# Neighbourhood keys stored as 64, meta, 384, meta, 64: nine transposes a head, and probabilities written over the biases

## The chip, the core and the metric

One core of a Trainium2 chip runs the whole program. Its engines are TensorE (PE, matmuls out of SBUF into PSUM), VectorE (DVE), ScalarE (ACT), GpSimd (POOL) and SyncE (SP), whose queue issues nearly all DMAs. Each engine takes its instructions in the order in which they were written into the program, and waits for others by semaphores. The metric is the time of one execution on the device in microseconds (us), the median of the runs.

## What is computed

Two layers of an encoder over 512 tokens (a grid of 8 rows and 64 columns) and 16 meta tokens, width 1024. A layer projects its normalised input with one large matrix, and its columns feed grouped-query attention (GQA), neighbourhood attention, and gates. The change touches neighbourhood attention: 8 heads of 64. A grid token sees the tokens of all 8 rows in a window of 16 columns, with a learned bias for each relative place, and the 16 meta keys; a meta token sees the meta keys alone.

```python
s_win  = einsum('bchd,bicjhd->bhcij', q_row, k_win) * scale + bias
s_meta = einsum('bchd,bmhd->bhcm', q_row, km) * scale
p = softmax(concatenate([s_win, s_meta], -1))
o = einsum('bhcij,bicjhd->bchd', p_win, v_win) + einsum('bhcm,bmhd->bchd', p_meta, vm)
o_meta = einsum('bhqm,bmhd->bqhd', softmax(s_mm), vm)
```

## The kernel before

Everything is float32. Each operand of a matmul is split into a high and a low part (`split`: a copy on ACT, a subtraction on DVE; for weights ACT and POOL), and three matmuls stand for one product (`product`, lines 309 to 311). The outer loop runs over chunks of 128 output columns of the projection; within a chunk over one or two ranges of tokens, of 264 or 512 columns, each into one of two PSUM banks (`ps_p`), then evacuated. After each range `tick()` moves two side streams on, one for neighbourhood heads (`side_na`) and one for GQA: a head is a list of steps, each with the number of ticks after the head's start (`NA_AT`). So the attention work is sown between the projections. A scheduler then sets each engine's order from the operations, their priorities (`tc.high_priority`) and the buffers.

Tokens are ordered by grid column, so a block of 128 queries covers 16 columns, and the keys that it needs are a contiguous run. The four blocks are in `BLK`: where the block's scores lie in a row of 960, its first key, and its number of keys (208, 272, 272, 208). Keys are stored with the 16 meta keys put in three times, 560 in all, so that each block's run holds one copy of them. The bias tile of a head (128 x 960, loaded in step `prepare`) has the same order.

A head's steps (`windowed_head`):

- `scores`: eight matmuls into a tile of two PSUM banks; DVE adds the bias and takes the maximum (line 874) into two tiles `Pb` of the shared set `B`; ACT takes the exponential; DVE and ACT scale.
- `transposes1` and `transposes2`: eight transposes on PE into the banks `ta` and `tb` (two banks, `ps_t`, serve all transposes of the kernel, GQA's `pt` and `ptm` too); `tb` has two narrow ones of 64 columns for the first and the last 64 keys. They are split into `tah`, `tal`, `tbh`, `tbl`; for the narrow ones `split_down` puts the low part on the partitions under the high one.
- `transposes3`: four transposes of 32 columns, one a block, of the stretch that holds its meta keys, into bank `tc`, split into `na` (128 x 512).
- `sums`: nine matmuls of these with the values `VB` into `avb`, then `combine`.

The values of a pair of heads are transposed in three calls (`window_values`): `vtb` (three of 128 tokens), `vtc` (two of 64), `vtd` (one of 32, with the meta tokens). In the rows, `pp` and `y` are projections, `whi` and `wlo` their weights, `vb` and `kb` values and keys of a pair, `S` and `P` GQA's scores and probabilities, `mm` and `tm` those of the meta queries, `avbm` their sum. Line numbers of the change are some 10 to 35 higher.

Of the kernel before, what the change touches and what calls it, by code (L numbers as in the profile page):

```python
# [11 lines left out]
F32 = mybir.dt.float32  # L12
# [14 lines left out]
NKEY = NTOK + 2 * NMETA  # L27
LAST = NTOK - P
HD = 64
# [7 lines left out]
NA_AT = ({"stages": (0, 2, 5, 5, 5, 7), "values": (3, 4, 6)},  # L37
         {"stages": (0, 2, 4, 5, 5, 7), "values": (3, 4, 5)})
# [14 lines left out]
BLK = ((0, 0, 208), (208, 64, 272), (480, 208, 272), (752, 352, 208))  # L53

BLK_META = (176, 112, 112, 176)


def _window_index():

    key = list(range(192)) + [-1] * 16 + list(range(192, 320)) + [-1] * 16 + list(range(320, 512)) + [-1] * 16  # L60
# [31 lines left out]
def trunk_kernel(ctx: ExitStack, tc: tile.TileContext, xT, w, gn, gf, bias, rope, out):  # L92
# [68 lines left out]
    for kind, (cols, n, dt) in {"ga": (256, 1, F32R), "na": (512, 1, F32R), "mm": (NMETA, 1, F32R), "pm": (32, 1, F32)}.items():  # L161
# [264 lines left out]
    for l in range(DEPTH):  # L426
# [197 lines left out]
        def keys_scaled():  # L624
# [46 lines left out]
        def values(v, out, tiles, name):
# [516 lines left out]
```

## Time and profile before

| what | value |
| --- | --- |
| median of 3 runs | 868.41 us (867.76 to 868.47) |
| the profiled execution | 869.61 us |
| its span, first to last instruction | 867.8 us |
| PE busy (matmuls) | 854.8 us, 99%, 5976 instructions |
| DVE busy | 537.2 us, 62% |
| ACT busy | 494.2 us, 57% |
| POOL busy | 365.6 us, 42% |
| chain that ended last | PE 86%, ACT 6%, DVE 4%, DMA 2% |
| PE clock granted | full in all 40 slices |

Busy times of PE count overlapping matmuls, so the share says that the queue is filled and not how fast it is worked off. That is read from the starts in the timeline. The rows are in a section further down.

### The profile page before, as it was taken

What the parts mean: (1) busy time and instruction counts of PE and PEld (TensorE: products, weight loads), DVE (VectorE), ACT (ScalarE), POOL (GpSimd) and SP (SyncE); (2) the same over time, 40 slices, a digit from 0 to 9 for tenths busy, and PEclk for the clock granted to TensorE, in tenths of its full rate; (3) what the DMA queues carried; (4) which work ended last, traced back from release to release, by engine and by line L of the source; (5) the groups of instructions that cost most, each with busy time, mean ns of one, the idle gap of its engine ahead of it and who ended that gap; (6) DMA issues with size and microseconds to landing.
All of it is one profiled execution on the core that took longest, in us unless ns stands there. A gap on an engine that the chain in (4) does not pass through costs nothing.

```text
span 867.8 us, 16234 instructions
## 1 busy us (share of the span) xinstructions
PE 854.8 (99%) x5976; PEld 790.6 (91%) x5976; DVE 537.2 (62%) x1277; ACT 494.2 (57%) x1170; POOL 365.6 (42%) x300
## 2 busy tenths in 40 slices
PE   8999999999999999999999999999999999999997
PEld 8999999999999999999998989898988888888786
DVE  5985667676774574436547656677767646454633
ACT  7645677677774555333445456677767645543432
POOL 5564323443223332544764643334333333334751
PEclk9999999999999999999999999999999999999999
DMA  6364253325112222325555664235422222223602
GB/s 223 99 186 145 93 150 99 106 73 153 49 50 75 62 67 81 98 86 152 148 139 127 171 198 130 79 95 151 145 81 73 86 73 73 87 85 97 206 25 97
DMA packets 64671, 95.76 MB, mean 110 GB/s; under 512 B 22864, under 2 KB 23376, under 8 KB 64592
## 3 DMA queue, kind: packets, MB, share of 16 engines
q1 hardware_dynamic: 63872, 93.66, 36.8%
q8 instruction: 47, 0.77, 0.4%
q10 hardware_dynamic: 720, 1.06, 0.3%
q14 instruction: 32, 0.26, 0.1%
HBM read 76.72 MB, written 4.19 MB: 93 GB/s over the span
## 4 chain that ended last, share of the span: by engine, by line
PE 86%; ACT 6%; DVE 4%; DMA 2%; issue 1%; POOL 0%; SPq 0%; POOLq 0%; ACTq 0%; DVEq 0%
PE pp L311 18%; PE pp L309 18%; PE pp L310 17%; PE y L309 4%; PE y L311 4%; PE y L310 3%; PE av L797 3%; PE pt L124 3%; PE avb L940 2%; PE pf L1115 2%; PE S L525 2%; PE pf L1117 2%; PE pf L1116 1%; PE S L526 1%; DMA x<-in_xT_dram 1%
## 5 line engine op out<-in xcount | busy, mean ns | idle before, releaser
L227 POOL TENSOR_TENSOR wlo<-raw,whi 128x512 fp32r<-128x512 f32 x214 | 285.3, 1337 | 425.4 <-ACT whi L226 341.7
L309 PE MATMUL pp<-hh,whi 128*128 128x264 f32 (+1 forms) x1056 | 334.7, 317 | 0.6 <-ACT qs L461 0.5
L311 PE MATMUL pp<-hh,wlo 128*128 128x264 f32 (+1 forms) x1056 | 329.3, 312 | 0.0
L310 PE MATMUL pp<-hl,whi 128*128 128x264 f32 (+1 forms) x1056 | 328.6, 311 | 0.0
L226 ACT CAST whi<-raw 128x512 fp32r<-128x512 f32 x214 | 131.5, 619 | 152.7 <-PE pp L310 58.3
L311 PEld LDWEIGHTS pp<-hh,wlo 128*128 128x128 f32 x1056 | 198.8, 188 | 10.7
L309 PEld LDWEIGHTS pp<-hh,whi 128*128 128x128 f32 x1056 | 198.6, 188 | 10.1 <-ACT qs L461 1.1
L310 PEld LDWEIGHTS pp<-hl,whi 128*128 128x128 f32 x1056 | 199.3, 189 | 9.0
L750 DVE CUSTOM_DVE_ANT_1 P<-S,r 128x528 f32<-128x528 f32 x64 | 45.1, 704 | 18.5 <-PE S L526 17.6
L183 DVE TENSOR_TENSOR ptl<-pt,pth 128x512 fp32r<-128x512 f32 x64 | 44.0, 689 | 18.0 <-ACT pth L182 17.2
L1012 DVE TENSOR_TENSOR mg<-pp,rbc 128x264 f32<-128x264 f32 (+1 forms) x48 | 24.8, 517 | 43.2 <-PE pp L311 42.7
L754 ACT ACTIVATE P<-P,st 128x528 f32<-128x528 f32 x64 | 47.2, 737 | 1.9
L876 ACT ACTIVATE Pb<-Pb,stb 128x208 f32<-128x208 f32 (+1 forms) x64 | 31.1, 487 | 16.6 <-DVE stb L874 16.3
L124 PE MATMUL pt<-ident,P 128*128 128x128 f32 x256 | 39.3, 275 | 0.6 <-DVE ptl L183 0.4
L182 ACT CAST pth<-pt 128x512 fp32r<-128x512 f32 x64 | 37.2, 583 | 4.2 <-PE pt L124 2.9
L1013 ACT ACTIVATE mg<-mg 128x264 f32<-128x264 f32 (+1 forms) x48 | 23.7, 494 | 24.4 <-DVE mg L1012 24.4
L310 PE MATMUL pp<-mx,whi 128*128 128x264 f32 x128 | 36.6, 286 | 0.0
L309 PE MATMUL pp<-mx,whi 128*128 128x264 f32 x128 | 36.4, 285 | 0.0
L311 PE MATMUL pp<-mx,wlo 128*128 128x264 f32 x128 | 36.3, 284 | 0.0
L797 PE MATMUL av<-pth,VA 128*128 128x256 f32 x128 | 35.0, 296 | 0.0
L756 DVE TENSOR_SCALAR P<-P,st 128x528 f32<-128x528 f32 x64 | 33.7, 527 | 2.1
L797 PE MATMUL av<-ptl,VA 128*128 128x256 f32 x128 | 33.1, 281 | 0.0
(526 smaller groups left out, 1764.3 us busy)
## 6 DMA issues: line engine op xcount, KB each, us to landing
raw<-in_w_dram SPq DMA_DIRECT2D x214, 256.0 KB, 2.7
bias<-in_bias_dram SPq DMA_DIRECT2D x16, 480.0 KB, 4.5
KB<-KB SPq DMA_DIRECT2D x24, 280.0 KB, 4.0
rawl<-in_w_dram SPq DMA_DIRECT2D x16, 256.0 KB, 2.9
x<-in_xT_dram SPq DMA_DIRECT2D x8, 264.0 KB, 6.3
xr<-in_xT_dram SPq DMA_DIRECT2D x8, 264.0 KB, 3.9
Q<-q SPq DMA_DIRECT2D x16, 128.0 KB, 2.9
x1d<-xt SPq DMA_DIRECT2D x32, 64.0 KB, 2.8
```

Of the source, the lines that this page charges most:

```text
L124: nc.tensor.transpose(ps, src, ident[:n, :n])
L182: split_at["hi"] = nc.scalar.copy(hi, src)
L183: split_at["any"] = nc.vector.tensor_sub(lo, src, hi.bitcast(F32))
L226: cast = nc.scalar.copy(hi, raw)
L227: sub = nc.gpsimd.tensor_sub(lo, raw, hi.bitcast(F32))
L309: nc.tensor.matmul(ps, wh, rh[:, a:b], start=i == 0, stop=False)
L310: nc.tensor.matmul(ps, wh, rl[:, a:b], start=False, stop=False)
L311: nc.tensor.matmul(ps, wl, rh[:, a:b], start=False, stop=i == n - 1)
L750: newest["max"] = nc.vector.tensor_tensor_reduce(p[:n].rearrange("p (i k) -> p i k", i=2), S[:n, :, :HALF], scale[:n].unsqueeze(2).to_broa ...
L754: nc.scalar.activation(p[:n], p[:n], AF.Exp, bias=st[:n, 1:2], scale=1.0, accum_out=st[:n, 2:3])
L756: nc.vector.tensor_scalar_mul(p[:n], p[:n], st[:n, 3:4])
L797: nc.tensor.matmul(c["av"], rows2(c["t"][i][0]), c["t"][i][1], start=i == 0, stop=i == 8)
```

## The change

The keys of a pair are stored as 64 tokens, 16 meta, 384 tokens, 16 meta, 64 tokens, 544 in all. Each block's run still holds one copy of the meta keys: the first two blocks use the first copy, the last two the second. In the first and the last block the meta keys lie beside the edge keys, so the two narrow transposes of `tb` take 80 columns, edge and meta together, and their low parts get a tile of their own instead of the lower partitions. In the bias tile the blocks stand in the order 0, 2, 1, 3; the ends of blocks 2 and 1 meet there, with the meta keys of both within 64 columns, and one transpose into `tc` serves both. Its tile `na` has 256 columns; the unwanted rows in it meet zeros in `VB`, made by a mask `inner`.

DVE writes the scores with bias, and ACT the exponentials, over the bias tile itself; the two tiles `Pb` are gone. The values of a pair are evacuated in the new order (`window_scaled`, five instructions for two), and the edges and meta values are transposed in one call (`window_edges`); `vtd` is a third transpose of `vtc`. `sums` has eleven matmuls; those of the edges use 80 rows and have a high and a low one each.

```diff
-NKEY = NTOK + 2 * NMETA
+NKEY = NTOK + NMETA
+EDGE = 64 + NMETA
...
           {"scores": (0, 1), "transposes": (3, 6), "meta": 6, "sums": (5, 7)})
-NA_AT = ({"stages": (0, 2, 5, 5, 5, 7), "values": (3, 4, 6)},
-         {"stages": (0, 2, 4, 5, 5, 7), "values": (3, 4, 5)})
+NA_AT = ({"stages": (0, 2, 5, 5, 5, 7), "values": (3, 4)},
+         {"stages": (0, 2, 4, 5, 5, 7), "values": (3, 4)})
...
-BLK = ((0, 0, 208), (208, 64, 272), (480, 208, 272), (752, 352, 208))
-BLK_META = (176, 112, 112, 176)
+BLK = ((0, 0, 208), (480, 64, 272), (208, 208, 272), (752, 336, 208))
+BLK_PS = ((0, 0), (0, 208), (1, 0), (1, 272))
+BLK_META = 448
 def _window_index():
-    key = list(range(192)) + [-1] * 16 + list(range(192, 320)) + [-1] * 16 + list(range(320, 512)) + [-1] * 16
+    key = list(range(64)) + [-1] * 16 + list(range(64, 448)) + [-1] * 16 + list(range(448, 512))
...
     padded = {}
-    for kind, (cols, n, dt) in {"ga": (256, 1, F32R), "na": (512, 1, F32R), "mm": (NMETA, 1, F32R), "pm": (32, 1, F32)}.items():
+    for kind, (cols, n, dt) in {"ga": (256, 1, F32R), "na": (256, 1, F32R), "mm": (NMETA, 1, F32R), "pm": (32, 1, F32)}.items():
...
         return padded[kind][0]
+    inner = cpool.tile([P, 1], F32, name="inner")
+    nc.gpsimd.memset(inner, 1.0)
+    nc.gpsimd.affine_select(inner, inner, pattern=[[0, 1]], compare_op=ALU.is_ge, fill=0.0, base=-NMETA, channel_multiplier=1)
+    nc.gpsimd.affine_select(inner, inner, pattern=[[0, 1]], compare_op=ALU.is_ge, fill=0.0, base=3 * NMETA - 1, channel_multiplier=-1)
...
-        def scaled(tag, c, name, full):
-            t = slot(tag, name) if tag != "bias" else slots.tile([P, 960], F32, tag=tag, bufs=2, name=name)
-            for ps, a, b in project(c, full):
+        def scaled(c, name):
+            t = slots.tile([P, 960], F32, tag="bias", bufs=2, name=name)
+            for ps, a, b in project(c, True):
                 evac["v"] = nc.vector.tensor_mul(t[:, a:b], ps, rbc[:, a:b])
-            if tag == "bias":
-                nc.vector.tensor_mul(t[:, NTOK:NTOK + NMETA], ps[:, b - a - NMETA:b - a], rbc[:, NREAL:NTOK])
-                nc.gpsimd.memset(t[:, NTOK + NMETA:NTOK + 2 * NMETA], 0.0)
+            nc.vector.tensor_mul(t[:, NTOK:NTOK + NMETA], ps[:, b - a - NMETA:b - a], rbc[:, NREAL:NTOK])
+            nc.gpsimd.memset(t[:, NTOK + NMETA:NTOK + 2 * NMETA], 0.0)
+            return t
+        def window_scaled(c, name):
+            t, e = slots.tile([P, NKEY], F32, tag="E", bufs=BUFS["E"], name=name), HD + 2 * NMETA
+            for ps, a, b in project(c, True):
+                r = rbc[:, a:b]
+                if a == 0:
+                    nc.vector.tensor_mul(t[:, :HD], ps[:, :HD], r[:, :HD])
+                    nc.vector.tensor_mul(t[:, e + HD:e + b], ps[:, HD:], r[:, HD:])
+                else:
+                    i, j = NREAL - HD - a, NREAL - a
+                    nc.vector.tensor_mul(t[:, e + a:], ps[:, :i], r[:, :i])
+                    nc.vector.tensor_mul(t[:, e:e + HD], ps[:, i:j], r[:, i:j])
+                    nc.vector.tensor_mul(t[:, HD:e].rearrange("p (i t) -> p i t", i=2),
+                                         ps[:, j:].unsqueeze(1).to_broadcast([P, 2, NMETA]),
+                                         r[:, j:].unsqueeze(1).to_broadcast([P, 2, NMETA]))
...
             split(out[:n, u:u + e, :, 0], out[:n, u:u + e, :, 1], src)
-            if n == 32 or e == 1 and n == 64:
-                for p in (slice(0, 16), slice(64, P))[:1 + (n == 32)]:
-                    nc.gpsimd.memset(out[p, u].rearrange("p h s d -> p (h s d)").bitcast(F32), 0.0)
             if n < P:
+                nc.gpsimd.memset(out[:NMETA, u].rearrange("p h s d -> p (h s d)").bitcast(F32), 0.0)
                 nc.scalar.copy(out[n:2 * n, u:u + e], out[:n, u:u + e].bitcast(F32))
-        v = scaled("bias", VA, f"va{l}", True)
+        def window_edges(v, out, name):
+            ps = bank(ps_t, f"vt{name}", "tp")
+            n, m = HD + NMETA, 4 * NMETA
+            for i in range(2):
+                nc.tensor.transpose(ps[:n, P * i:P * (i + 1)], v[:, n * i:n * (i + 1)], ident)
+            nc.tensor.transpose(ps[:m, 2 * P:3 * P], v[:, HD - NMETA:HD - NMETA + m], ident)
+            src = ps[:, :3 * P].rearrange("p (t h d) -> p t h d", t=3, h=2)
+            split(out[:n, 4:6, :, 0], out[:n, 4:6, :, 1], src[:n, :2])
+            hi, lo = out[:m, 0, :, 0], out[:m, 0, :, 1]
+            with tc.high_priority():
+                nc.scalar.mul(hi, src[:m, 2], inner[:m])
+                nc.vector.scalar_tensor_tensor(lo, src[:m, 2], inner[:m], hi.bitcast(F32), op0=ALU.mult, op1=ALU.subtract)
+            nc.scalar.copy(out[m:2 * m, 0], out[:m, 0].bitcast(F32))
+        v = scaled(VA, f"va{l}")
...
                 st = tiny.tile([P, 3, 4], F32, tag="stb", bufs=3, name=f"stb{nm}")
-                p = [slot("B", f"Pb{nm}_{i}") for i in range(2)]
-                pb = [p[b // 2][:, base - 480 * (b // 2):base - 480 * (b // 2) + n] for b, (base, k0, n) in enumerate(BLK)]
-                c["p"] = pb
+                pb = c["p"] = [c["bias"][:, base:base + n] for base, k0, n in BLK]
                 stacks["scored"] += 1
                 for b, (base, k0, n) in enumerate(BLK):
-                    i, c0 = b // 2, base - 480 * (b // 2)
+                    i, c0 = BLK_PS[b]
                     score(S[:, i, c0:c0 + n], c["q"], c["k"], slice(P * b, P * (b + 1)), slice(k0, k0 + n))
                 for b, (base, k0, n) in enumerate(BLK):
-                    i, c0 = b // 2, base - 480 * (b // 2)
+                    i, c0 = BLK_PS[b]
                     if b == 2:
                         nc.vector.reciprocal(st[:, 2, :2], st[:, 1, :2])
                     with tc.high_priority():
-                        nc.vector.tensor_tensor_reduce(pb[b], S[:, i, c0:c0 + n], c["bias"][:, base:base + n], -1.0, 3e38,
+                        nc.vector.tensor_tensor_reduce(pb[b], S[:, i, c0:c0 + n], pb[b], -1.0, 3e38,
...
-                    score(ps, c["q"], c["k"], slice(NREAL, NTOK), slice(NKEY - NMETA, NKEY))
+                    score(ps, c["q"], c["k"], slice(NREAL, NTOK), slice(HD, HD + NMETA))
...
             def transposes1():
                 pb = c["p"]
                 tp = bank(ps_t, f"ta{nm}", "tp")
-                for i, (b, o0) in enumerate(((0, 64), (1, 0), (1, 144), (2, 0))):
+                for i, (b, o0) in enumerate(((0, 80), (1, 16), (1, 144), (2, 0))):
...
                     nc.vector.tensor_copy(mh[:32], ps)
-                    nc.vector.tensor_sub(mh[32:64], ps, mh[:32].bitcast(F32))
+                    nc.vector.tensor_sub(mh[64:96], ps, mh[:32].bitcast(F32))
                     c["mt"] = mh
             def transposes2():
                 pb = c["p"]
                 tp = bank(ps_t, f"tb{nm}", "tp")
-                transposed(tp[:, 0:P], pb[2][:, 144:272])
+                transposed(tp[:, 0:P], pb[2][:, P:2 * P])
                 transposed(tp[:, P:2 * P], pb[3][:, 0:P])
-                transposed(tp[:64, 2 * P:3 * P], pb[0][:, 0:64])
-                transposed(tp[:64, 3 * P:4 * P], pb[3][:, P:P + 64])
+                transposed(tp[:EDGE, 2 * P:3 * P], pb[0][:, :EDGE])
+                transposed(tp[:EDGE, 3 * P:4 * P], pb[3][:, P:P + EDGE])
                 c["b"] = bh, bl = slot("B", f"tbh{nm}", F32R), slot("B", f"tbl{nm}", F32R)
                 split(bh[:, :256], bl[:, :256], tp[:, :256])
-                split_down(bh, tp[:64, 256:512], 64, 256, 512)
+                split(bh[:EDGE, 256:512], bl[:EDGE, 256:512], tp[:EDGE, 256:512])
             def transposes3():
-                pb = c["p"]
                 tp = bank(ps_t, f"tc{nm}", "tp")
-                for b in range(4):
-                    transposed(tp[:32, P * b:P * (b + 1)], pb[b][:, BLK_META[b]:BLK_META[b] + 32])
-                c["m"] = pad_tile("na")
-                split_down(c["m"], tp[:32], 32, 0, 512)
+                transposed(tp[:64, :P], c["bias"][:, BLK_META:BLK_META + 64])
+                c["m"] = tm = pad_tile("na")
+                split_meta([(tm[:, P:2 * P], tp[:, :P]), (tm[:, :P], tp[:, :P])])
             def sums():
                 VB2, o = kvq[j]["v2"], kvq[j]["o"]
                 av = bank(ps_a, f"avb{nm}", "avn")
-                seq = [(0, c["m"], 0, 0, 512)]
+                seq = [(0, c["m"], 0, 128, 384)]
                 for t in c["a"]:
                     seq += [(1, t, 0, 0, 256), (2, t, 256, 128, 384)]
-                bh, bl = c["b"]
-                seq += [(4, bh, 256, 0, 128), (5, bh, 384, 384, 512), (3, bh, 0, 256, 512), (3, bl, 0, 256, 512)]
+                for t in c["b"]:
+                    seq += [(3, t, 0, 256, 512), (4, t, 256, 0, 128), (5, t, 384, 384, 512)]
                 for i, (u, t, c0, a, b) in enumerate(seq):
-                    nc.tensor.matmul(av[:, a:b], rows2(VB2[:, u, hh]), t[:, c0:c0 + b - a], start=i == 0,
+                    r = slice(0, EDGE if u > 3 else P)
+                    nc.tensor.matmul(av[:, a:b], rows2(VB2[r, u, hh]), t[r, c0:c0 + b - a], start=i == 0,
...
                 kvq[j]["o"] = slot("B", f"ob{l}_{j}")
-            tiles = ([(1, 64, P), (2, 192, P), (3, 320, P)], [(4, 0, 64), (5, 448, 64)], [(0, NTOK - 32, 32)])[i]
-            values(vb, kvq[j]["v2"], tiles, f"{'bcd'[i]}{l}_{j}")
+                values(vb, kvq[j]["v2"], [(t, 32 + P * t, P) for t in range(1, 4)], f"b{l}_{j}")
+            else:
+                window_edges(vb, kvq[j]["v2"], f"c{l}_{j}")
...
+                r = rbc[:, a:b]
                 if a == 0:
-                    nc.vector.tensor_mul(kb[:, 0:192], ps[:, 0:192], rbc[:, 0:192])
-                    nc.vector.tensor_mul(kb[:, 208:16 + HALF], ps[:, 192:HALF], rbc[:, 192:HALF])
+                    nc.vector.tensor_mul(kb[:, :HD], ps[:, :HD], r[:, :HD])
+                    nc.vector.tensor_mul(kb[:, EDGE:NMETA + b], ps[:, HD:], r[:, HD:])
                 else:
-                    nc.vector.tensor_mul(kb[:, 16 + HALF:336], ps[:, :320 - HALF], rbc[:, HALF:320])
-                    nc.vector.tensor_mul(kb[:, 352:544], ps[:, 320 - HALF:NREAL - HALF], rbc[:, 320:NREAL])
-                    for o in (192, 336, NKEY - NMETA):
-                        nc.vector.tensor_mul(kb[:, o:o + 16], ps[:, NREAL - HALF:HALF], rbc[:, NREAL:NTOK])
+                    i, e = NREAL - HD - a, NREAL - a
+                    nc.vector.tensor_mul(kb[:, NMETA + a:NKEY - EDGE], ps[:, :i], r[:, :i])
+                    nc.vector.tensor_mul(kb[:, NKEY - HD:], ps[:, i:e], r[:, i:e])
+                    for o in (HD, NKEY - EDGE):
+                        nc.vector.tensor_mul(kb[:, o:o + NMETA], ps[:, e:], r[:, e:])
             kvq[j]["k_done"] = True
...
-            kvq[j]["v"] = scaled("E", VB + j, f"vb{l}_{j}", True)
+            kvq[j]["v"] = window_scaled(VB + j, f"vb{l}_{j}")
```

The order of PE at the transposes of head 2 in layer 0, between the matmuls of a projection chunk (`pp_12`), before:

```order
L309 MATMUL pp_12_0_2149<-hh_2_166,whi_12_0_2008 128x264
L124 MATMUL tb_2_2107<-ident,Pb_2_1_1866 128x128 x2
L124 MATMUL tb_2_2107<-ident,Pb_2_0_1865 64x128
L124 MATMUL tb_2_2107<-ident,Pb_2_1_1866 64x128
L310 MATMUL pp_12_0_2149<-hl_2_167,whi_12_0_2008 128x264
L311 MATMUL pp_12_0_2149<-hh_2_166,wlo_12_0_2009 128x264
L309 MATMUL pp_12_0_2149<-hh_3_171,whi_12_0_2008 128x264
L124 MATMUL tc_2_2118<-ident,Pb_2_0_1865 32x128 x2
L124 MATMUL tc_2_2118<-ident,Pb_2_1_1866 32x128 x2
L310 MATMUL pp_12_0_2149<-hl_3_172,whi_12_0_2008 128x264
L311 MATMUL pp_12_0_2149<-hh_3_171,wlo_12_0_2009 128x264
```

and with the change:

```order
L322 MATMUL pp_12_0_2150<-hh_0_141,wlo_12_0_2009 128x264
L129 MATMUL tb_2_2109<-ident,bias_2_1747 128x128 x2
L129 MATMUL tb_2_2109<-ident,bias_2_1747 80x128 x2
L320 MATMUL pp_12_0_2150<-hh_1_152,whi_12_0_2008 128x264
L321 MATMUL pp_12_0_2150<-hl_1_153,whi_12_0_2008 128x264
L322 MATMUL pp_12_0_2150<-hh_1_152,wlo_12_0_2009 128x264
L320 MATMUL pp_12_0_2150<-hh_2_170,whi_12_0_2008 128x264
L321 MATMUL pp_12_0_2150<-hl_2_171,whi_12_0_2008 128x264
L322 MATMUL pp_12_0_2150<-hh_2_170,wlo_12_0_2009 128x264
L320 MATMUL pp_12_0_2150<-hh_3_175,whi_12_0_2008 128x264
L129 MATMUL tc_2_2120<-ident,bias_2_1747 64x128
L321 MATMUL pp_12_0_2150<-hl_3_176,whi_12_0_2008 128x264
```

`tb` stands four matmuls earlier there, with 80 columns for its narrow ones, and `tc` is one instruction.

DVE at the same place, before (`P` is GQA's score step, an ISA row, and the second ISA row its maximum):

```order
L908 CAST mm_124<-tm_2_2103 32x16
L183 TENSOR_TENSOR tal_2_2100<-ta_2_2094,tah_2_2099 128x512
L750 ISA P_1_1_1980,st_1_1_1_2130<-S_1_1_1_2125,r_0_827 128x528
L750 ISA st_1_1_1_2130 128x1
L909 TENSOR_TENSOR mm_124<-tm_2_2103,mm_124 32x16
L183 TENSOR_TENSOR tbl_2_2113<-tb_2_2107,tbh_2_2112 128x256
L755 RECIPROCAL st_1_1_1_2130<-st_1_1_1_2130 128x1
L756 TENSOR_SCALAR P_1_1_1980<-P_1_1_1980,st_1_1_1_2130 128x528
L730 TENSOR_TENSOR na_122<-tc_2_2118,na_122 32x512
L730 TENSOR_TENSOR tbh_2_2112<-tb_2_2107,tbh_2_2112 64x256
```

and with the change:

```order
L940 CAST mm_124<-tm_2_2105 32x16
L941 TENSOR_TENSOR mm_124<-tm_2_2105,mm_124 32x16
L783 ISA P_1_1_1980,st_1_1_1_2131<-S_1_1_1_2126,r_0_831 128x528
L783 ISA st_1_1_1_2131 128x1
L194 TENSOR_TENSOR tal_2_2102<-ta_2_2096,tah_2_2101 128x512
L194 TENSOR_TENSOR tbl_2_2115<-tb_2_2109,tbh_2_2114 128x256
L788 RECIPROCAL st_1_1_1_2131<-st_1_1_1_2131 128x1
L789 TENSOR_SCALAR P_1_1_1980<-P_1_1_1980,st_1_1_1_2131 128x528
L194 TENSOR_TENSOR tbl_2_2115<-tb_2_2109,tbh_2_2114 80x256
L771 TENSOR_TENSOR na_122<-tc_2_2120,na_122 32x128 x2
```

`tal`, the low part of `ta`, moved behind the score step of GQA, and the second `mm` ahead of it; `na` is two instructions of 128 columns for one of 512, behind the edges.

SP's queue in layer 0, about the bias load of head 2, before:

```order
L856 DMA bias_2_1746<-in_bias_dram 128x960
L224 DMA raw_23_1_1542<-in_w_dram 128x512
L224 DMA raw_7_0_1700<-in_w_dram 128x512
L224 DMA raw_7_1_1706<-in_w_dram 128x512
L224 DMA raw_16_0_1824<-in_w_dram 128x512
L504 DMA KB_11_1660<-KB_10_1659 64x1120 x2
L856 DMA bias_3_2051<-in_bias_dram 128x960
L504 DMA KB_10_1659<-KB_10_1659 64x1120
```

and with the change:

```order
L235 DMA raw_23_1_1547<-in_w_dram 128x512
L235 DMA raw_7_0_1701<-in_w_dram 128x512
L235 DMA raw_7_1_1707<-in_w_dram 128x512
L235 DMA raw_16_0_1824<-in_w_dram 128x512
L889 DMA bias_2_1747<-in_bias_dram 128x960
L515 DMA KB_11_1659<-KB_10_1658 64x1088 x2
L515 DMA KB_10_1658<-KB_10_1658 64x1088
L235 DMA raw_16_1_1830<-in_w_dram 128x512
```

The load of head 2 moved behind four weight loads (`raw`); that of head 3 moved from between the key transfers (`KB`) to behind these rows.

## Rows read from the trace of the kernel before

**Rows 1.** The page, part 1: engine, busy us, share of the span, instructions.

```profile
PE 854.8 (99%) x5976; PEld 790.6 (91%) x5976; DVE 537.2 (62%) x1277; ACT 494.2 (57%) x1170; POOL 365.6 (42%) x300
```

**Rows 2.** Waits of PE and its weight loads: releaser, us in total, times, longest.

```profile
PE vtd L676 <- DVE na L730: 1.3, 4, 0.7
PE tb L124 <- DVE tal L183: 0.2, 1, 0.2
...
PEld vtd L676 <- DVE na L730: 3.1, 5, 1.1
PEld tc L124 <- DVE tal L183: 1.2, 6, 0.2
```

**Rows 3.** Timeline of PE at four narrow transposes: start us, us, engine, line, operation.

```profile
142.21 0.28 PE L309 MATMUL pp<-hh,whi 128*128 128x264 f32 x1
142.33 0.60 PE L124 MATMUL tc<-ident,Pb 128*32 128x128 f32 x4
142.68 0.37 PE L310 MATMUL pp<-hl,whi 128*128 128x264 f32 x1
142.89 0.28 PE L311 MATMUL pp<-hh,wlo 128*128 128x264 f32 x1
```

**Rows 4.** Timeline of PE at a single transpose of 64 columns.

```profile
264.48 0.27 PE L124 MATMUL ptm<-ident,P 128*64 128x128 f32 x1
264.51 0.37 PE L309 MATMUL y<-ob,whi 128*128 128x264 f32 x1
264.71 0.28 PE L310 MATMUL y<-ob,whi 128*128 128x264 f32 x1
```

**Rows 5.** Timeline of PE at the sums of a head.

```profile
111.15 0.39 PE L940 MATMUL avb<-na,VB 128*128 128x512 f32 x1
111.38 0.39 PE L940 MATMUL avb<-tah,VB 128*128 128x256 f32 x2
...
111.85 0.52 PE L940 MATMUL avb<-tbh,VB 128*128 128x128 f32 x3
112.20 0.28 PE L940 MATMUL avb<-tbl,VB 128*128 128x256 f32 x1
112.32 0.17 PE L951 MATMUL avbm<-mm,VB 128*128 128x16 f32 x1
112.34 0.37 PE L525 MATMUL S<-KA0h,Q 128*128 128x264 f32 x1
112.55 0.28 PE L526 MATMUL S<-KA0l,Q 128*128 128x264 f32 x1
```

**Rows 6.** Timeline of PE at the longest wait of `vtd`.

```profile
666.52 0.39 PE L309 MATMUL pp<-hh,whi 128*128 128x512 f32 x1
667.61 0.29 PE L676 MATMUL vtd<-ident,vb 128*32 128x128 f32 x1 [0.69 <-DVE na L730]
667.65 0.48 PE L310 MATMUL pp<-hl,whi 128*128 128x512 f32 x1
```

**Rows 7.** Groups by line and shape, DVE: count, busy us, mean ns, idle before.

```profile
L738 DVE TENSOR_TENSOR ga<-ptm,ga 32x128 fp32r<-32x128 f32 x64 | 18.2, 285 | 6.7 <-ACT ga L736 5.4
L1012 DVE TENSOR_TENSOR mg<-pp,rbc 128x264 f32<-128x264 f32 x32 | 13.8, 431 | 30.7 <-PE pp L311 30.4 <-PE vtd L676 0.2
L1012 DVE TENSOR_TENSOR mg<-pp,rbc 128x512 f32<-128x512 f32 x16 | 11.0, 690 | 12.4 <-PE pp L311 12.4
L730 DVE TENSOR_TENSOR na<-tc,na 32x512 fp32r<-32x512 f32 x16 | 10.9, 680 | 4.5 <-ACT na L729 4.3
```

**Rows 8.** Timeline: `tc` of head 0 on PE, head 2's first biases on DVE.

```profile
103.33 0.61 PE L124 MATMUL tc<-ident,Pb 128*32 128x128 f32 x4
...
125.26 0.38 DVE L874 CUSTOM_DVE_ANT_0 Pb<-Sb,bias 128x208 f32<-128x208 f32 x1 [0.40 <-PE sm L526]
```

**Rows 9.** The page, part 6: DMA issues, count, KB each, us to landing.

```profile
bias<-in_bias_dram SPq DMA_DIRECT2D x16, 480.0 KB, 4.5
```

**Rows 10.** Waits of SP's queue: the longest entry of the bias loads.

```profile
SPq L856 <- DVE stb L872: 14.0, 6, 5.3
```

More of the change, by code (lines that the diff above doesn't have):

```diff
@@ L109, in slot @@
     def slot(tag, name, dt=F32):
-        n = NKEY if tag in ("KB", "KR") else NTOK + NMETA if tag == "K" else NTOK
-        return slots.tile([P, n], dt, tag=tag, bufs=BUFS[tag], name=name)
+        n = NKEY if tag in ("KB", "KR", "K", "E") else NTOK
+        t = slots.tile([P, n], dt, tag=tag, bufs=BUFS[tag], name=name)
+        return t[:, :NTOK] if tag == "E" else t
     def two(tag, name, dt=F32):
@@ L630, in keys_scaled @@
             nc.tensor.transpose(ps[:, :P], st["fm"][:, 0], ident)
-            nc.vector.tensor_mul(k[:, NREAL:], k[:, NREAL:], ps[:, P - NMETA:P])
             both_ends = keys[0]
-            nc.vector.tensor_copy(both_ends[:, :NMETA], k[:, NREAL:])
+            for t in (both_ends[:, :NMETA], k[:, NREAL:]):
+                nc.vector.tensor_mul(t, k[:, NREAL:], ps[:, P - NMETA:P])
             KA2.extend(stack_soon("K", f"KA{l}", both_ends, NTOK + NMETA, 0))
@@ L724, in rows2 @@
             return v.rearrange("p s d -> p (s d)")
-        def split_down(t, tp, rows, a, b):
-            with tc.high_priority():
-                nc.scalar.copy(t[:rows, a:b], tp)
-                nc.vector.tensor_sub(t[rows:2 * rows, a:b], tp, t[:rows, a:b].bitcast(F32))
         def split_meta(parts):
```

## The prediction

> **What bounds the kernel now.** I read the page first. TensorE (PE) is busy 99% of the span [rows 1], and the reader is to take this as "the queue of matmuls is nearly never empty", not as work at full speed, since matmuls overlap. So I looked next at what PE waits for [rows 2]: the whole list of its idle gaps is short, and the longest entry of the part of the program that the change touches is `vtd`, the transpose of the meta values, which waits for VectorE (DVE) to finish `na`. No entry names a weight tile, a bias or a key stack. Last I read PE's timeline for the distance from one start to the next, which is what an instruction costs a full queue; the durations in the rows (0.28 us for 264 columns) overlap and are no price. A projection matmul follows its neighbour after 0.12 us [rows 3, 4]. The kernel's time is therefore PE's sum of such distances plus a few waits, and an instruction taken off PE is worth its distance, wherever in the neighbourhood part it stands. Work on DVE, ScalarE (ACT), GpSimd and the DMA queues counts only where PE comes to wait for it.
>
> **Transposes.** Each of the 16 heads (8 in each of two layers) loses three: `tc` was four of 32 columns and is one of 64; `ta` and `tb` keep four each, `tb`'s edges 80 columns for 64. Price: from the matmul ahead of four `tc` to the second one behind them is 0.68 us (142.21 to 142.89), in which two projection matmuls take 0.24, so 0.44 for four, 0.11 each [rows 3]. A single 64-column one: 264.48 to 264.71 is 0.23 for it and one matmul, so again 0.11 [rows 4]. Both rows agree, so a lone one in the place of four is not dearer. 48 x 0.11 = 5.3 us off PE. The values of a pair keep six transposes; only their calls are joined.
>
> The Trainium skill, "TensorE: Matmul & The Clock Gate", section "LDWEIGHTS (loading the stationary operand)", says that a weight load's time goes with its columns, 128 columns over 1.2 GHz being 107 ns, so 27 ns for 32. By that price alone the old four `tc` would have been nearly free, and the sum below would end near rival one. The trace does not agree that this sets the distance: four loads of 32 columns took 0.44 us on PE.
>
> **Matmuls of the sums (`avb`).** Before, nine a head: one of 512 columns, six of 256, two of 128. After, eleven: seven of 256 and four of 128. Distances in one head [rows 5]: 0.23 for the 512 (111.15 to 111.38); 0.12 for a 256 (112.20 to 112.32); the three `tbh` take 0.35, so the two of 128 share 0.23, 0.115 each. The 512 that becomes a 256 saves 0.11; two more of 128 cost 0.23; net +0.12 a head, 16 x 0.12 = +1.9 us. That the edges now contract 80 rows is shown by no row. The nearest are the 128-row ones here and the 16-column `avbm`, which with the next matmul takes 0.23 (112.32 to 112.55), so 0.11: small ones do not get cheaper. Per added matmul 0.105 to 0.125, I take 0.115; that is 1.6 to 2.2 for the term.
>
> **The wait of `vtd`.** It is gone as an instruction of its own: the meta values are now the third transpose of `vtc`, one step earlier. Its PSUM bank in layer 1 was the one that `tc` had just left, so it waited for DVE's `na` behind `tc`. In the longest case 666.52 to 667.61 is 1.09 where the 512-column matmul takes 0.23, so 0.86 lost, against 0.69 idle on PE's row and 1.1 on the weight loads' [rows 2, 6]. Scaling the two totals by that case, 1.3 x 0.86 / 0.69 = 1.6 and 3.1 x 0.86 / 1.1 = 2.4; I take 2.0. The lower end is nothing, if the next user of that bank waits as long. Against this: the next user, GQA's `pt`, stands behind the sums' first part and more projection matmuls, and `na` itself is shorter: one DVE subtraction of 680 ns becomes two of 285 [rows 7].
>
> **Waits that stay, move or come.** `tc`'s own wait for `tal` (1.2 us over 6 on the weight loads, [rows 2]) stays: `ta`, `tb` and their banks are as before. In head 2 of layer 0 the order puts `tb` four matmuls earlier and `tal` behind the softmax step of GQA. The built program gives this `tb` the bank that `tm` leaves, so it waits for the small `mm` and no longer for `tal` (0.2 idle, [rows 2]); I count -0.3, and +1.0 as the other end, if `tal` held it. In the last head of layer 1 `tb` comes one 512-column matmul earlier while it still waits for `ptl`: +0.2 (0.23, [rows 5]; 0 to 0.5).
>
> DVE: the values of a pair were evacuated in two instructions of 264 columns and are in five (64, 200; 184, 64, 32). From 431 ns at 264 and 690 at 512 columns [rows 7] an instruction has 155 fixed and 1.04 a column; three more and 16 columns are +0.48 us a pair, of which 0.33 in the second half. The keys lose one instruction and 16 columns, -0.17; the two heads' `na` give back 2 x 0.11. DVE's work is about level (+0.1 a pair); only its timing differs. Where the 0.33 stands ahead of a softmax that PE waits for, it costs: at most 8 pairs x 0.33 = 2.6, and nothing (or -0.5, by the shorter `na`) where DVE is ahead. PE waits for DVE in few places, so I take +0.3. ACT loses a copy of 64x512 a pair, and POOL two memsets: both off the path, and no PE wait in rows 2 names them. The setup of `inner` on POOL replaces a memset there: nothing.
>
> **Probabilities over the biases.** The bias load of head n+2 now waits for `tc` of head n instead of its score step, and SP holds whatever stands behind it. The cover: the order moves the load behind the weight loads that are due first; the shortest of the twelve distances is in layer 0, `tc` at 103.33 to the next use of that tile at 125.26, 22 us [rows 8], against 4.5 us of landing [rows 9]. Waits of bias loads up to 5.3 us stand already in SP's queue [rows 10] and no PE wait on weights came of them. Nothing; without that cover it would be the length of SP's wait, weight loads included.
>
> **Sum.** -5.3 + 1.9 - 2.0 - 0.3 + 0.2 + 0.3 = -5.2 us. The profiled execution took 869.61 us (span 867.8), 1.2 above the median of the runs, 868.41. So 864.4 for such an execution, 863.2 for the median. All lower ends together (-5.3 + 1.6 - 2.4 - 0.3 + 0.0 - 0.5) give -6.9, 861.5; all upper ends together (-5.3 + 2.2 + 0 + 1.0 + 0.5 + 2.6) +1.0, 869.4. That all upper ones meet is unlikely.
>
> **Rivals.**
> One: the removed transposes were cheap, a quarter of 0.11 since they loaded 32 of 128 columns. Then -1.3 for -5.3, and the sum is -1.2: 867.2. Rows 3 speak against it; for it, only that one distance there carries the reading.
>
> Two: the waits come back. `vtd`'s 2.0 goes to the next user of the bank and the values' second half costs its 2.6: -5.2 + 2.0 + 2.3 = -0.9: 867.5. For it: PE's waits on DVE are nearly all on such a two-bank rotation. Against: the next users stand several matmuls later. In this case the change does less than it says: fewer instructions, same waits.
>
> Three, slower: DVE comes one subtraction late in every head. PE would wait at `tc` or at the sums for one more DVE instruction of 0.69 us (the 680 of `na`, [rows 7]), 16 x 0.69 = 11.0, so +5.8 in all: 874.2. It decides from 5.2 / 16 = 0.33 us a head. For it: five evacuations for two beside the transposes' splits in layer 0. Against: DVE's sum is level and `na` shorter.
>
> **How the numbers follow.** Forecast 0.77, rival one 0.07, two 0.09, three 0.07. The forecast's own spread is 861.3 to 866.6 (0.2 below the lower ends for readings of two digits; upwards about half of the way from the sum to the upper ends). To hold 8 in 10 the range takes in rival one: 861.3 to 867.2. A measurement here can tell 0.2%, 1.7 us, from no change: the forecast is faster (0.77), rivals one and two lie within it (0.16), three is slower (0.07).
>
> **What would show it.** PE's instructions fall by 16: 48 transposes fewer, 32 matmuls of 128 columns more. Right: one `tc` a head with about 0.35 us between its neighbours (0.24 + 0.11); `avb` from first to last start about 0.1 longer; no `vtd` among PE's waits and no new name above 1 us in total; head 2's `tb` with no wait for `tal`. Wrong, if `tc` alone costs more than 0.11 or four of 80 rows drop below 0.1; if `pt`, `sm` or `ta` show PE waits on `na`, `tbl` or `VB`; if SP waits on `tc` and a weight tile enters PE's list; or if the softmax rows behind `vb` move PE by more than 1 us.

## The result, and the profile after

| | before | changed |
| --- | --- | --- |
| median of 6 runs | 868.53 us (867.76 to 869.32) | 863.22 us (862.94 to 863.72) |
| the profiled execution | 869.61 us | 862.94 us |
| its span | 867.8 us | 861.2 us |

The ratio is 0.9939 (95% interval 0.9926 to 0.9952): 5.3 us faster, where 5.2 were forecast. The page's line for PE, which answers to [rows 1]:

```profile
PE 849.1 (99%) x5960; PEld 788.7 (92%) x5960; DVE 533.4 (62%) x1309; ACT 491.6 (57%) x1178; POOL 360.6 (42%) x287
```

16 instructions fewer, as forecast. What PE waits for (releaser, us in total, times, longest), then its weight loads; this answers to [rows 2]:

```profile
PE pt L129 <- DVE P L789: 0.9, 1, 0.9
PE tc L129 <- DVE VB L722: 0.8, 1, 0.8
PE tb L129 <- DVE ptl L194: 0.7, 1, 0.7
...
PE avb L973 <- DVE tbl L194: 0.2, 1, 0.2
```

```profile
PEld tc L129 <- PE tb L129: 1.0, 1, 1.0
PEld tc L129 <- DVE tal L194: 0.8, 3, 0.3
```

`vtd` is gone, and `tc` stands there with a new releaser, `VB` of line 722. Two more entries are new or longer: `pt`, which waited 0.2 us for `P` before, and `avb` with `tbl`. Each of the three is under 1 us on PE; what they cost is read below.

**Where in the run the time went.** The two profiled executions differ by 6.6 us of span, more than the medians by 1.3. The place of the difference is seen at the first transpose `ta` of layer 0 (PE timeline, before and then changed):

```profile
101.20 0.60 PE L124 MATMUL ta<-ident,Pb 128*128 128x128 f32 x4
```

```profile
99.91 0.60 PE L129 MATMUL ta<-ident,bias 128*128 128x128 f32 x4
```

Up to this row PE's order is the same in both programs but for one transpose, and yet the changed kernel is 1.29 us ahead. In the twelve profiles of this study the row stands between 99.63 and 101.99 us, and what the kernels do there doesn't explain it: two kernels with the same PE instructions throughout (changed, and e6 below) have it at 99.91 and 101.17. Before that point PE waits for the first loads, splits and softmaxes; behind it distances repeat to 0.1 us. So I compare what lies behind it, the span less this row: 766.6 us before, 761.3 changed, **5.3 less**. That agrees with the medians, and it is what the experiments below call the rest. (The changed kernel has one transpose more ahead of the row, so 0.1 us of it has only moved there.)

One wait ahead of the row sets the changed kernel apart: `pt` at 72.29 us, which waits 0.9 us for the scaled probabilities `P`. ACT's exponential in front of them stands behind the split of a weight, and that waits for the weight's load (ACT, before and then changed):

```profile
71.31 0.62 ACT L226 CAST whi<-raw 128x512 fp32r<-128x512 f32 x1 [2.23 <-DMA raw<-in_w_dram]
```

```profile
69.91 0.62 ACT L237 CAST whi<-raw 128x512 fp32r<-128x512 f32 x1 [2.96 <-DMA raw<-in_w_dram]
```

In the traces of the experiments below this `pt` waits 0.4 to 1.4 us in e1, e2, e5 to e8 and f2, and 0.2 in e3 and e4; in f1 a score matmul ahead of it waits 2.2 us instead. So it goes with the probabilities written over the biases, which e2 has alone, and not with the values. Why the load lands later there, no run shows.

**Transposes.** PE's timeline at `tb` and `tc` of a head of layer 1 where nothing waits, before:

```profile
544.36 0.60 PE L124 MATMUL tb<-ident,Pb 128*128 128x128 f32 x4
544.80 0.60 PE L124 MATMUL tc<-ident,Pb 128*32 128x128 f32 x4
545.15 0.36 PE L797 MATMUL av<-pth,VA 128*128 128x256 f32 x1
545.35 0.28 PE L797 MATMUL av<-ptl,VA 128*128 128x256 f32 x1
```

and changed:

```profile
539.62 0.60 PE L129 MATMUL tb<-ident,bias 128*128 128x128 f32 x4
540.05 0.27 PE L129 MATMUL tc<-ident,bias 128*64 128x128 f32 x1
540.08 0.36 PE L830 MATMUL av<-pth,VA 128*128 128x256 f32 x1
540.28 0.28 PE L830 MATMUL av<-ptl,VA 128*128 128x256 f32 x1
```

From `tb` to the second matmul behind `tc` it was 544.36 to 545.35, 0.99 us, and is 539.62 to 540.28, 0.66: 0.33 for three transposes, 0.11 each.

**Sums.** The same head as in [rows 5], changed:

```profile
109.31 0.28 PE L973 MATMUL avb<-na,VB 128*128 128x256 f32 x1
...
109.90 0.46 PE L973 MATMUL avb<-tbh,VB 128*128 128x256 f32 x3
110.20 0.50 PE L973 MATMUL avb<-tbl,VB 128*128 128x256 f32 x3
...
110.62 0.37 PE L536 MATMUL S<-KA0h,Q 128*128 128x264 f32 x1
```

From the first `avb` to the matmul behind `avbm` it is 109.31 to 110.62, 1.31; before, 111.15 to 112.34, 1.19 [rows 5]. That is +0.12 in this head. To the second matmul behind the sums the median of the eight heads grew by 0.11 in either layer (1.36 to 1.47 and 1.28 to 1.40). The last head of layer 0 has 0.45 more: there DVE subtracts the edges' part of `tbl` behind GQA's scaling, and PE waits for it. That is the entry `avb` in the list above.

**The new wait.** PE, DVE and ACT at the last pair of layer 1, changed:

```profile
657.68 0.60 PE L129 MATMUL tb<-ident,bias 128*128 128x128 f32 x4
659.09 0.27 PE L129 MATMUL tc<-ident,bias 128*64 128x128 f32 x1 [0.81 <-DVE VB L722]
```

```profile
657.39 0.40 DVE L194 TENSOR_TENSOR VB<-vtc,VB 80x256 fp32r<-80x256 f32 x1
...
658.19 0.50 DVE L789 TENSOR_SCALAR P<-P,st 128x528 f32<-128x528 f32 x1
658.60 0.34 DVE L722 SCALAR_TENSOR_TENSOR VB<-vtc,inner,VB 64x128 fp32r<-64x128 f32 x1
```

```profile
655.57 0.37 ACT L193 CAST VB<-vtc 80x256 fp32r<-80x256 f32 x1
...
657.14 0.74 ACT L787 ACTIVATE P<-P,st 128x528 f32<-128x528 f32 x1
...
657.87 0.35 ACT L721 ACTIVATE VB<-vtc,inner 64x128 fp32r<-64x128 f32 x1
```

`tc` takes the bank that `vtc` leaves. That bank is free when the last of `vtc`'s four evacuations ends. ACT copied the edges at 655.57 and was then idle, but the meta values' high part (line 721) stands behind the exponential of GQA (line 787), and their low part on DVE (line 722) behind GQA's scaling (line 789). So `tc` starts at 659.09, 0.97 us later than the distance of four transposes from 657.68 would put it. In this pair `vtd` lost 0.86 before [rows 6]: to `na`, at another place, and about as much.

### The profile page after: what moved, and what is told of

It reads as the page before. It is cut to its first block, busy times and chain, and to the rows that moved or that the text cites. A ratio compares the mean times of both kernels' runs of the same rounds, so it can differ in the third digit from the quotient of the medians.

```text
span 861.2 us, 16238 instructions
## 1 busy us (share of the span) xinstructions
PE 849.1 (99%) x5960; PEld 788.7 (92%) x5960; DVE 533.4 (62%) x1309; ACT 491.6 (57%) x1178; POOL 360.6 (42%) x287
## 3 DMA queue, kind: packets, MB, share of 16 engines
q10 hardware_dynamic: 720, 1.06, 0.3%
## 5 line engine op out<-in xcount | busy, mean ns | idle before, releaser
L908 ACT ACTIVATE bias<-bias,stb 128x208 f32<-128x208 f32 (+1 forms) x64 | 31.1, 486 | 24.1 <-DVE stb L906 23.8
```

## Experiments

"Rest" is the span less the start of the first `ta`. All ran beside the kernel before (medians 868.48 to 868.66).

| run | median us | first `ta` | span | rest | rest against its base |
| --- | --- | --- | --- | --- | --- |
| before | 868.53 | 101.20 | 867.8 | 766.6 | |
| changed | 863.22 | 99.91 | 861.2 | 761.3 | -5.3 |
| e1, three more `tc` of 32 | 868.76 | 100.51 | 867.1 | 766.6 | +5.3 to changed |
| e8, three more of 128 | 868.43 | 100.04 | 866.6 | 766.6 | +5.3 to changed |
| e7, no low edges | 860.59 | 100.24 | 858.5 | 758.3 | -3.0 to changed |
| e5, `tal` twice | 865.49 | 99.63 | 862.8 | 763.2 | +1.9 to changed |
| e6, meta values first | 863.50 | 101.17 | 862.7 | 761.5 | +0.2 to changed |
| f1, one split | 863.14 | 101.99 | 862.9 | 760.9 | -0.4 to changed |
| f2, f1 with a later `tb` | 867.76 | 100.01 | 866.0 | 766.0 | +5.1 to f1 |
| e2, in place | 868.68 | 100.94 | 867.4 | 766.5 | -0.1 to before |
| e3, `vtd` joined | 866.87 | 99.87 | 864.7 | 764.8 | -1.8 to before |
| e4, values in five | 868.37 | 100.27 | 866.6 | 766.3 | -0.3 to before |

**e1 and e8: what a transpose costs.** In the changed kernel:

```diff
                 transposed(tp[:64, :P], c["bias"][:, BLK_META:BLK_META + 64])
+                for b in range(1, 4):
+                    transposed(tp[:32, P * b:P * (b + 1)], c["bias"][:, BLK_META:BLK_META + 32])
```

and in e8 the same three with 128 columns each.

> The changed kernel (863.2) with three more transposes of 32 columns in each of the 16 heads, right behind the one into tc, into columns of that bank that nobody reads. No splits, no matmuls of the sums are added. If a transpose costs PE 0.11 us whatever its columns (the forecast), 48 x 0.11 = +5.3: 868.5, and 0.44 us between tc's neighbours where it was 0.11. If a narrow one costs a quarter (rival one), +1.3: 864.5.

> As the run with three more transposes of 32 columns a head (868.76), but the three take 128 columns of the probabilities each; nobody reads them. If PE's price is the instruction, the same: 868.5 to 868.8, and 0.44 us between tc's neighbours. If the columns loaded count at all (four times as many here), the 48 cost more than the narrow ones' 5.5: with 0.08 more for 96 more columns, +3.8: 872.5.

Measured: +5.5 and +5.2 by the medians, +5.3 in the rest of both. PE's timeline of e8 at the head shown above:

```profile
542.48 0.60 PE L129 MATMUL tb<-ident,bias 128*128 128x128 f32 x4
542.92 0.60 PE L129 MATMUL tc<-ident,bias 128*64 128x128 f32 x4
543.27 0.36 PE L830 MATMUL av<-pth,VA 128*128 128x256 f32 x1
```

From `tb` to the first matmul behind `tc` it is 0.79 us (542.48 to 543.27), as before the change (544.36 to 545.15), against 0.46 in the changed kernel (539.62 to 540.08). 48 transposes cost 5.3 us, 0.11 each, with 32 columns as with 128: rival one falls. The rule of the Trainium skill ("TensorE: Matmul & The Clock Gate", section "LDWEIGHTS (loading the stationary operand)") that a load's time goes with its columns does not set PE's distance here.

**e7: what an edge matmul costs.** In the changed kernel:

```diff
-                for t in c["b"]:
-                    seq += [(3, t, 0, 256, 512), (4, t, 256, 0, 128), (5, t, 384, 384, 512)]
+                for t, parts in zip(c["b"], (3, 1)):
+                    seq += [(3, t, 0, 256, 512), (4, t, 256, 0, 128), (5, t, 384, 384, 512)][:parts]
```

> The changed kernel (863.2) without the two matmuls of a head that take the low parts of the edges' probabilities (80 rows, 128 columns), so that part of the sum is left out. If such a matmul costs PE 0.11 us though it contracts 80 rows and not 128, 32 x 0.11 = -3.5: 859.7. If it goes with its rows (80/128 of 0.11 = 0.07), -2.2: 861.0. If it hides behind its neighbours (0.03, as avbm's distance behind the sums), -1.0: 862.2.

Measured 860.59, and the rest fell by 3.0: between the first and the second theory. The sums say which: from the first `avb` to the second matmul behind the sums, the median head went from 1.47 to 1.24 in layer 0 and from 1.40 to 1.17 in layer 1, 0.23 for two, so 0.11 each, 3.6 in all. Some 0.4 of it came back as a longer wait of `tc` in one head (PE's waits of e7):

```profile
PE tc L129 <- DVE VB L722: 1.2, 2, 0.8
```

(0.8 over 1 in the changed kernel.) Another 0.6 came back at `pt` and `ptm` in layer 0, while the sums' wait of 0.45 for `tbl` went. Contracting 80 rows made these matmuls no cheaper than the 0.115 us of those that contract 128 [rows 5].

**e3: `vtd` alone.** In the kernel before, with the two splits of `vtc` and of the meta values in one call:

```diff
-NA_AT = ({"stages": (0, 2, 5, 5, 5, 7), "values": (3, 4, 6)},
-         {"stages": (0, 2, 4, 5, 5, 7), "values": (3, 4, 5)})
+NA_AT = ({"stages": (0, 2, 5, 5, 5, 7), "values": (3, 4)},
+         {"stages": (0, 2, 4, 5, 5, 7), "values": (3, 4)})
...
+            for i, a in enumerate((0, 448)):
+                nc.tensor.transpose(ps[:64, P * i:P * (i + 1)], v[:, a:a + 64], ident)
+            nc.tensor.transpose(ps[:32, 2 * P:3 * P], v[:, NTOK - 32:NTOK], ident)
```

> The kernel before (868.5) with one part of the change alone: the transpose of the meta values is a third one of the call vtc, in its bank, and vtd is gone; keys, the four narrow tc and the sums are as before. Forecast of the prediction: vtd's waits go and nothing takes their place, -2.0: 866.5. Rival two: tc, which takes the bank that vtc leaves, waits in its place; in the changed kernel tc's waits grew by 1.1 where vtd's fell by 2.2, so -1.1: 867.4. If all of it comes back, 868.5.

Measured 866.87, ratio 0.9982 (0.9973 to 0.9991), so 0.8 to 2.3 us faster; the rest fell by 1.8, of which 0.1 is a transpose that moved ahead of the first `ta`. The time alone can't decide between the forecast and rival two. The trace can: a wait at `tc` comes, though keys and `tc` are those of before (PE's waits of e3):

```profile
PE tc L124 <- DVE VB L183: 0.7, 1, 0.7
```

So joining the call takes away the five waits of `vtd`, 2.2 us by starts, and 1.1 come back at `tc`, 0.9 of it in this one place. It is this part of the change that brings the new wait, not the key layout. The rest falls by more than the 1.1 left over, in part because `ptm` waits 0.3 less for `ptl`.

**e6 and f1: what the new wait hangs on.** In e6 the meta values' two instructions are written ahead of the edges':

```diff
-            split(out[:n, 4:6, :, 0], out[:n, 4:6, :, 1], src[:n, :2])
             hi, lo = out[:m, 0, :, 0], out[:m, 0, :, 1]
             with tc.high_priority():
...
+            split(out[:n, 4:6, :, 0], out[:n, 4:6, :, 1], src[:n, :2])
```

> The changed kernel (863.2) with the two instructions that split the meta values written ahead of the two that split the edges, in the same call; nothing else differs, and PE's order is the same. In the last pair of layer 1, tc waits 0.97 us for the masked low part, whose high part ACT makes behind the exponential of GQA. If the wait of vtd came back there as a wait on this order, it goes: -0.8 to -0.9, 862.4, and tc's distance there falls from 1.08 to 0.2 or less. If tc waits for whatever leaves that bank last, the edges' split takes its place: 863.2.

The second case: 863.5, and the wait stayed. DVE and PE of e6 at that place:

```profile
658.74 0.33 DVE L721 SCALAR_TENSOR_TENSOR VB<-vtc,inner,VB 64x128 fp32r<-64x128 f32 x1
...
659.54 0.50 DVE L789 TENSOR_SCALAR P<-P,st 128x528 f32<-128x528 f32 x1
659.95 0.41 DVE L194 TENSOR_TENSOR VB<-vtc,VB 80x256 fp32r<-80x256 f32 x1
```

```profile
659.04 0.60 PE L129 MATMUL tb<-ident,bias 128*128 128x128 f32 x4
660.51 0.27 PE L129 MATMUL tc<-ident,bias 128*64 128x128 f32 x1 [0.87 <-DVE VB L194]
```

Now the meta values leave early (658.74) and the edges' low part stands behind GQA's scaling (659.95): ACT takes one copy of `vtc` before the exponential, whichever it is. In f1 there is one copy for all:

```diff
-            split(out[:n, 4:6, :, 0], out[:n, 4:6, :, 1], src[:n, :2])
...
-                nc.scalar.mul(hi, src[:m, 2], inner[:m])
-                nc.vector.scalar_tensor_tensor(lo, src[:m, 2], inner[:m], hi.bitcast(F32), op0=ALU.mult, op1=ALU.subtract)
...
+            split(out[:n, 3:6, :, 0], out[:n, 3:6, :, 1], src[:n])
+            flat = out[:m, 3].rearrange("p h s d -> p (h s d)")
+            nc.gpsimd.tensor_scalar_mul(flat, flat.bitcast(F32), inner[:m])
...
```

The meta values' transpose takes 80 columns there, as the edges' do, and the parts of `VB` are numbered to match.

> The changed kernel (863.2) in which edges and meta values of a pair leave their bank by one ACT copy and one DVE subtraction of 80x384 instead of two each, and POOL sets the unwanted rows to zero afterwards. In the run with the meta values first the edges' pair of instructions took the place of the meta's behind GQA's softmax. If tc in the last pair of layer 1 waits for the second pair of instructions whichever it is, there is none now: tc's distance there falls from 1.08 to about 0.2, -0.9 in that stage: 862.3. If tc waits for something else there, 863.2.

DVE and PE of f1 there:

```profile
659.69 0.54 DVE L194 TENSOR_TENSOR VB<-vtc,VB 80x384 fp32r<-80x384 f32 x1
```

```profile
660.00 0.60 PE L129 MATMUL tb<-ident,bias 128*128 128x128 f32 x4
660.43 0.27 PE L129 MATMUL tc<-ident,bias 128*64 128x128 f32 x1
```

`tc` starts right behind `tb`: the wait is gone, as expected. The time hardly moved: 863.14 against 863.22. By PE's starts against those of the changed kernel, f1 gains 1.3 us in layer 1 up to and with this pair, but loses 0.5 in layer 0, where more `tc` wait for `tal`, and 0.3 behind the pair, where `tb` of the last head waits longer for `ptl`. What remains, 0.4 in the rest, no median here can tell from nothing.

**f2: a later `tb`.** f1 with `"stages": (0, 2, 4, 6, 6, 7)` for layer 1.

> The kernel with one split (f1), with tb and tc of layer 1 one tick later (6 for 5). In the last head of layer 1 tb waits 0.83 us for ptl, the low part of GQA's probabilities that leaves that bank. If a tick later that bank is free, -0.8 more: 861.5. Against it: the sums stand at tick 7, and with tc one tick closer PE waits for tbl or na in up to eight heads; at 0.3 each +2.4: 864.7.

867.76: the case against it, at another place and twice the price. PE's largest wait in f2:

```profile
PE pt L129 <- DVE na L768: 3.9, 5, 1.4
```

`pt`, GQA's transpose, now follows `tc` into the same bank and waits for `na` in five heads, up to 1.4 us; `tb` still waits for `ptl`. This is rival two's mechanism, larger than in any other run, made by one tick.

**e5: DVE late in every head.** In the changed kernel:

```diff
                 split(c["a"][0][:, :512], c["a"][1][:, :512], tp)
+                with tc.high_priority():
+                    nc.vector.tensor_sub(c["a"][1][:, :512], tp, c["a"][0][:, :512].bitcast(F32))
```

> The changed kernel (863.2) in which DVE writes tal, the low part of ta, twice in each head: 16 more subtractions of 0.69 us (about 0.6 from start to start) right where tc and tb wait for that bank. Rival three, that PE follows DVE in every head: 16 x 0.6 = +9.6: 872.8. The forecast, that DVE is ahead except where tc waits for tal already (six heads of layer 0, none of layer 1): 6 x 0.6 = +3.6: 866.8, all of it in layer 0.

865.49, +2.3 by the medians and +1.9 in the rest. Rival three's 9.6 is four to five times too much; the 3.6 was too much as well and in the wrong place, since the added instruction moves others in the schedule. The waits are at `pt` (layer 0) and at `tc` and `tb` (layer 1):

```profile
PE pt L129 <- DVE VB L194: 1.2, 2, 0.7
...
PE tc L129 <- DVE VB L722: 0.9, 2, 0.7
...
PE tb L129 <- DVE tal L936: 0.6, 1, 0.6
```

Of 16 x 0.6 us of DVE, PE sees about a fifth, 0.1 us for a subtraction on average; single places still lose up to 0.8 (`pt` in layer 0).

**e2: in place alone.** In the kernel before:

```diff
-                p = [slot("B", f"Pb{nm}_{i}") for i in range(2)]
-                pb = [p[b // 2][:, base - 480 * (b // 2):base - 480 * (b // 2) + n] for b, (base, k0, n) in enumerate(BLK)]
+                pb = [c["bias"][:, base:base + n] for base, k0, n in BLK]
```

> The kernel before (868.5) with one part of the change alone: scores with bias and exponentials are written over the bias tile, the tiles Pb are gone; keys, transposes, sums and values are as before. The bias load then waits for tc two heads earlier. Forecast: the wait lies under 22 us of cover, no PE wait on a weight appears, 868.5 within 0.5. Against it: SP holds weight loads behind the bias loads; then PE's list of waits names whi or wlo and the time rises by 1 us or more, 869.5 up.

868.68, ratio 0.9996 (0.9987 to 1.0005), rest -0.1. SP's queue does wait for `tc` now, at two loads of the last projection's weights, which go into the bias tiles, and at the biases:

```profile
SPq L218 <- PE tc L124: 6.2, 2, 3.6
...
SPq L856 <- PE tc L124: 3.0, 6, 1.2
```

PE's waits name no weight, and behind the first `ta`, where every `tc` stands, no distance on PE grew by 0.1 us or more: the cover holds. But the list has the wait of `pt` that stands behind a weight's load (0.2 in the kernel before):

```profile
PE pt L124 <- DVE P L756: 1.3, 1, 1.3
```

It lies ahead of the first `ta` and of any `tc`, so the wait for `tc` is not its reason. The medians show no time for this part of the change that is clear of the noise.

**e4: the values' evacuation alone.** In the kernel before:

```diff
-                evac["v"] = nc.vector.tensor_mul(t[:, a:b], ps, rbc[:, a:b])
+                for c0, c1 in ((a, b),) if tag == "bias" else ((0, 64), (64, b)) if a == 0 else ((a, 448), (448, 512), (512, b)):
+                    evac["v"] = nc.vector.tensor_mul(t[:, c0:c1], ps[:, c0 - a:c1 - a], rbc[:, c0:c1])
```

> The kernel before (868.5) with one thing alone: the values of a pair are evacuated in five DVE instructions (64 and 200, then 184, 64 and 16 columns) instead of two of 264, to the same places. PE's order is that of before. By 155 ns fixed an instruction that is +0.47 us of DVE a pair. The prediction's term: +0.3 in all, 868.8. Its upper end, that each pair's second half reaches PE: 8 x 0.33 = +2.6, 871.1. If DVE is always ahead: 868.5.

868.37, ratio 0.9996 (0.9988 to 1.0005), rest -0.3: nothing clear of the noise. The instructions themselves cost what the prediction worked out. In the changed kernel (operations on `vb`: least, median and largest ns):

```profile
L686 DVE TENSOR_TENSOR vb<-pp,rbc x8: 208/225/225, 65.3 to 622.0; 128x64 f32<-128x64 f32 x8
L687 DVE TENSOR_TENSOR vb<-pp,rbc x8: 351/356/358, 65.4 to 622.1; 128x200 f32<-128x200 f32 x8
L690 DVE TENSOR_TENSOR vb<-pp,rbc x8: 339/350/350, 67.9 to 625.9; 128x184 f32<-128x184 f32 x8
L691 DVE TENSOR_TENSOR vb<-pp,rbc x8: 213/214/216, 68.2 to 626.1; 128x64 f32<-128x64 f32 x8
L692 DVE TENSOR_TENSOR vb<-pp,rbc x8: 179/182/187, 69.0 to 626.3; 128x32 f32<-128x32 f32 x8
```

Summed 1.33 us a pair, against 2 x 0.433 before: +0.46, forecast +0.48. Behind the first `ta` no wait of PE grew by more than about 0.2 us.

## Why the prediction was right, and where it was not

| term | forecast | measured | by |
| --- | --- | --- | --- |
| transposes | -5.3 | -5.3 | 0.33 a head; e1, e8 |
| sums | +1.9 | +1.8 | 0.11 a head; e7 |
| wait of `vtd` | -2.0 | -1.1 | 2.2 gone, 1.1 back at `tc` |
| `tb` in head 2 of layer 0 | -0.3 | -0.3 | no wait there |
| `tb` in the last head | +0.2 | +0.15 | its wait 0.68, now 0.83 |
| `ptm` behind `ptl` | none | -0.4 | 0.9 lost in three places before, 0.5 now |
| sums behind `tbl` | none | +0.45 | last head of layer 0 |
| DVE | +0.3 | none seen | e4 |
| what remains | | about -0.6 | to make -5.3 |

The waits are sums over PE's starts: each distance less that of the same instruction in a full queue. The last line is a difference, with all errors in it; 0.1 of it is the transpose that moved ahead of the first `ta`, and the rest of e2 and e4, whose PE order is that of before, differs by 0.1 and 0.3 from it. What else it holds stays open.

- **Transposes and sums** are the whole of the sure gain, 3.5 of 5.3, and right as they were worked out: by the distance in a full queue. The sign "`avb` from first to last start about 0.1 longer" came out at 0.06 (medians 1.06 to 1.12 and 1.05 to 1.11); the other 0.05 falls on the matmuls behind.
- **The wait of `vtd`** was mis-sized. What was taken off was about right (2.2 by starts, forecast 2.0). "The next user stands several matmuls later" was said of GQA's `pt`. But the meta values moved a step forward, and there the next user of their bank is `tc`, four transposes behind. In that pair rival two was right; e3 shows it by itself.
- **DVE.** The cost of 0.3 that was forecast for the values' evacuation doesn't show (e4). Two effects of DVE's order that no term had do show: `ptm` waits 0.4 less, the sums wait 0.45 more.
- **Luck.** The forecast of 863.2 stands so close to 863.22 because errors cancelled: 1.35 too little at `vtd` and at the sums' wait, against 0.4 at `ptm`, 0.3 for DVE and the 0.6 that remains. Its small terms are good to about 1 us, no better.
- **The in-place step** costs nothing that the medians show (e2), and at `tc` the cover was there as worked out. But the prediction looked for harm from the wait for `tc` alone; the `pt` that waits behind a weight's load ahead of the first `ta` was not foreseen, and its reason is open. **Rival one** fell by e1 and e8, **rival three** by e5.
- The profiled execution of before was taken as 1.2 us above the median as a whole. By the rests it was the start of the run: behind the first `ta` the kernel before (766.6) is level with e2 and e4 (766.5 and 766.3), which were profiled nearer to their medians.

No version with the whole sum beat the changed kernel by more than its runs differ: f1's 863.14 is the same time.

## What to carry to other kernels

Where one queue is full, price an instruction by the start-to-start distance of its like in the trace, not by its duration or size: it held here to a tenth of a microsecond over 48 instructions. When a step that fills a rotating bank is moved or joined, list who takes that bank next at the *new* place and what stands ahead of its last evacuation on each engine; half of the waits removed at one place came back at the next one here, and in f2 a move by one tick made 3.9 us of them. And compare two traces from a landmark behind the first loads on, but read the stretch ahead of it as well: it differed by over 2 us between the profiles, and it held a wait that goes with the change.

## What the runs showed of the hardware

A weight load's duration grew less than its columns. Operations on `vb` in the kernel before (least, median, largest ns), 128 columns, 64 and 32:

```profile
L676 PEld LDWEIGHTS vtb<-ident,vb x24: 137/139/142, 92.7 to 656.0; 128*128 128x128 f32 x24
...
L676 PEld LDWEIGHTS vtc<-ident,vb x16: 108/110/112, 97.3 to 660.5; 128*64 128x64 f32 x16
...
L676 PEld LDWEIGHTS vtd<-ident,vb x8: 93/95/97, 105.7 to 667.6; 128*32 128x32 f32 x8
```

A quarter of the columns takes 95 ns for 139. And the distance on PE didn't follow size either: 0.11 us for transposes of 32, 64 and 128 columns ([rows 3, 4], e8), and about as much for matmuls of 128 columns whether they contract 80 rows or 128 (e7, [rows 5]). A matmul of 512 columns, though, took 0.23.
